# A decoder layer on one core: the last head's turn two row blocks later, its small steps in another order, and the gate sums one projection later

## Chip, cores and metric

The kernel runs on one core of a Trainium2 chip. The metric is the device time of one execution in microseconds (us). The kernel before took 787.35, 786.34 and 785.03 us in three runs, median 786.34.

## The reference

One layer maps 512 tokens of width 1024 to the same shape. A vector c gives six modulation rows (shift, scale and gate for two branches) through a 1024x6144 matrix. The first branch mixes tokens in two groups, whose outputs are joined and projected:

```
mod = silu(c) @ ada_w + ada_b               # 6 x 1024
u   = rms_norm(x) * (1 + scale) + shift
z   = u @ w_in                              # q, k, v, o, gates | a, b
# group 1: four mLSTM heads of width 256
lf  = log_sigmoid(f);  F = cumsum(lf);  m = running max(i - F)
s   = (q @ k.T) / 16 * exp(F_t - F_s + i_s - m_t)     # causal
h   = s @ v / max(|sum(s)|, exp(-m));  h = rms_norm(h) * sigmoid(o)
# group 2: GLU, causal depthwise convolution of width 31, layer norm, silu
y   = silu(layer_norm(conv(a * sigmoid(b))))
x1  = x + gate * rms_norm(concat(h, y) @ w_out)
# second branch: up to 2 x 2816, convolution of width 3, gated, down, gate
```

All is float32. Products are taken in three parts: each factor is split into a high and a low part (names ending in h and l), and high x high, low x high and high x low are added.

## The kernel before, in words

PE (TensorE) and SP (SyncE) work in the order in which the code is written. DVE (VectorE), ACT (ScalarE) and POOL (GpSimd) are ordered by a scheduler: it goes by priorities (raising `tc.cur_priority` by LATER makes what follows yield to the rest), by dependencies added by hand that only order two instructions on one engine (`add_manual_dep`, and `behind` for short), and inside `in_order()` by the code.

*Head 0 and the gates.* `head_proj(0, j)` (six calls) is one projection block of 24 products for q, k and o of the first head; the profile's products qko_0, qko_1 and so on. Between them stand the gate steps: `fcum` sums the log forget gates over tokens with eight small products (L752), DVE copies the sums (Fc, L754) and forms ga (L755), `aT` turns ga (L761), and DVE scans it. `g_lf`, which fcum reads, is the end of a chain of small DVE steps (L709 to L713) that stand between the convolution's taps (`cv`, L900). Those taps run on DVE through the whole first half.

*Head 3, the last.* `attention(h)` is a generator (L631 on) whose parts are put between other products by `next(steps)`: scores s (L639) and their scaling E on DVE (L640), the outputs o (L650), then per token tile a copy to hn and a sum of squares ssq on ACT. Then come the small steps, all 128x4: dm (L662), its reciprocal rd (L663), two steps on ssq (L664, L665) on DVE, ssq plus epsilon and its power fac on POOL (L666, L667), and for the last head fac times rd on DVE (L669). ACT scales hn by fac (L673, four copies), PE turns it (hT, L682: eight 128x128 transposes into two banks), and ACT and DVE split the turned rows into hh and hl (L692, L693).

*The output projection.* `mix_first(n)` multiplies row block n of w_out (wo_n, 128 rows, 12 products, n from 0 to 9) into the banks mixa; blocks 0 to 7 read the convolution group (yh, yl), blocks 8 and 9 the last head (hh, hl). The other heads go through products of sums (names m, ms, mt; Strassen-like) into mixa and mixb. Each raw block is loaded by SP; ACT makes the high part, POOL the low part (`w_split`, L199 and L200). After blocks 8 and 9 come wo1's ten blocks (the right half of the columns) into mixb.

*The modulation sums.* `ada_block(i)` loads a 128x1024 block of the transposed modulation matrix on ACT's queue (L177) and multiplies it by c with a sum along the row on DVE (`junk`, L182). 48 such blocks make mod; 20 to 39 are done while the last head and the output projection run. `gain` forms gains from mod; `send_rows` turns gains on PE (gT, L786), copies them on DVE (gTs, L789) and writes them to memory on ACT's queue (row_d, L791); `row` loads them back to all partitions (g1r, L797), after the write has landed. DVE multiplies mixa by g1r (mg).

Of the kernel before, what the change touches and what calls it, by code (L numbers as in the profile page):

```python
# [10 lines left out]
F32 = mybir.dt.float32  # L11
# [3 lines left out]
ALU = mybir.AluOpType  # L15
# [42 lines left out]
def decoder_layer(ctx, tc, w_glu0, x, c, adaT, vecs, w_glu, w_qko, w_v0, w_vo, w_mq, w_out, w_up, w_down, out):  # L58
# [46 lines left out]
    def atbank(name):  # L105
        return psum.tile([P, T], F32, tag="at", bufs=2, name=name)
# [63 lines left out]

    def ada_block(i, behind, load_behind=None):

        if i % 6 < 4 and 24 <= i < 40:
            r = spare[0][:, 2 * (i % 6) : 2 * (i % 6) + 2, :].rearrange("p j t -> p (j t)")
        else:
            r = adas.tile([P, D], F32, tag="ada", name=f"ada_{i}")
        load = nc.scalar.dma_start(r, adaT[i // 2][:, (i % 2) * D : (i % 2 + 1) * D])  # L177
        if load_behind is not None:
            tc.add_manual_dep(load.ins, load_behind.ins.name, mybir.DependencyInfo(mybir.DependencyClass.NoSync, mybir.DependencyReason.DATA),
                              reason="order on ScalarE")  # L180
        junk = small.tile([P, D], BF16, tag="junk", bufs=1, name=f"junk_{i}")
# [11 lines left out]
    def w_split(src, name, pool=None, tag="w", eng=None):  # L193

        n = src.shape[1]
        pool = pool or wpool
        hi = pool.tile([P, T], F32R, tag=tag, name=f"{name}h")
        lo = pool.tile([P, T], F32R, tag=tag, name=f"{name}l")
        S.activation(hi[:, :n], src, AF.Copy)  # L199
        last_w[0] = (eng or G).tensor_tensor(out=lo[:, :n], in0=src, in1=hi[:, :n].bitcast(F32), op=ALU.subtract)  # L200
        return hi, lo
# [363 lines left out]
    def head_proj(h, i):  # L565

        pieces, qs, ks, so = heads[h]
        ps = mmbank(f"qko{h}_{i}")
        proj(ps, pieces, i * KT)
        e = 2 * h + i % 2  # L570
        if i < 2:
            qs.append(conv4(ps, e, f"q{h}_{i}"))
        elif i < 4:
            ks.append(conv4(ps, 8 + e, f"k{h}_{i}"))
        else:
            t = slot(f"so{h}_{i}")
            S.activation(t, ps, AF.Tanh, scale=0.5)
            so.append(t)
# [49 lines left out]
        yield  # L628
        tc.cur_priority += LATER

    def attention(h):  # L631

        _, qs, ks, so = heads[h]

# [31 lines left out]
        G.tensor_scalar(out=ssq, in0=ssq, scalar1=EPS, scalar2=None, op0=ALU.add)  # L666
        last_fac[0] = G.tensor_tensor(out=fac, in0=ssq, in1=mhalf, op=ALU.pow)  # L667
        if h == H - 1:
            V.tensor_tensor(out=fac, in0=fac, in1=rd, op=ALU.mult)  # L669
# [6 lines left out]
        yield  # L676
        turned_h = []
        for e in range(2):
            tp = (mmbank if h < 2 else atbank)(f"hT{h}_{e}")
            for tt in range(NT):  # L680
                src = hn[tt // 2][:, (tt % 2) * DH + e * P : (tt % 2) * DH + (e + 1) * P]
                PE.transpose(tp[:, tt * P : (tt + 1) * P], src, ident)  # L682
# [9 lines left out]
            S.activation(hi, t, AF.Copy, scale=g)  # L692
            last_lo[0] = V.scalar_tensor_tensor(out=lo, in0=t, scalar=g, in1=hi.bitcast(F32), op0=ALU.mult, op1=ALU.subtract)  # L693
            hy[2 * h + e] = (hi, lo)
# [58 lines left out]
    Fc, ga = g16("Fc"), g16("ga")  # L753
    V.tensor_copy(Fc, fv)  # L754
    V.tensor_tensor(out=ga, in0=gz[:, :, :H], in1=Fc, op=ALU.subtract)  # L755
    head_proj(0, 2)

    head_proj(0, 3)
    aps = atbank("aT")
# [23 lines left out]
    def send_rows(a, n, queue=nc.scalar):  # L783

        ps = atbank(f"gT{a}")
        PE.transpose(ps[:n, :P], gains[:, a : a + n], ident)  # L786
        t = side(f"gTs{a}") if a == 3 * KT else slot(f"gTs{a}") if a == 0 else vpool.tile([P, 2 * T + 8], F32, tag="vh", name=f"gTs{a}")
        t = t[:, :P]
        V.tensor_copy(t[:n, :], ps[:n, :P])  # L789
        for i in range(n // KT):  # L790
            queue.dma_start(rows_d[a // KT + i].rearrange("(j p) -> j p", p=P), t[i * KT : (i + 1) * KT, :])  # L791
# [49 lines left out]

    def wo_split(r, n, i):
        wo[n + i] = w_split(r[:, i * T : (i + 1) * T], f"wo0_{n + i}")

    def mix_first(n, tts=range(NT)):
        if n not in wo:
# [18 lines left out]
            ts = slice(off + q * P, off + (q + 1) * P)  # L865
            mm3(ps, (hi[:, ts], lo[:, ts]), w[p], start and p == 0, p == PAIRS - 1, True)

    last_kept = [None]

    def kept(banks, name):  # L870
        out = [cvtile(f"{name}{q}") for q in range(2)]
        last_kept[0] = S.activation(out[0], banks[0], AF.Copy)
        V.tensor_copy(out[1], banks[1])
        return out

    ys = [None] * KT
# [102 lines left out]
    for h in range(H - 1):  # L979
# [48 lines left out]
        if h == H - 2:  # L1028
            norm_sums()

    tc.cur_priority += LATER
    for i in range(16, 20):
        ada_block(i, scaled)
    for i in range(20, 24):
        ada_block(i, last_left[0])
    ada_done(16, 24)
    gain(0, 16, "mix_post_g")
    tc.cur_priority -= LATER
    wo = {}
    steps = attention(H - 1)  # L1040
    low, high = mixa[:2], mixa[2:]
    s14 = upool.tile([P, KT, T], F32R, tag="uh", name="ms14")
    norm_factor()
# [41 lines left out]
        next(steps)  # L1085
    mix_first(0)
    next(steps)
    for p in range(PAIRS):
        sums_split(p, "14", (s14[:, 2 * p, :], s14[:, 2 * p + 1, :]))
    for n in range(1, 6):  # L1090
        mix_first(n)
    spare.append(upool.tile([P, KT, T], F32, tag="ul", name="spare"))
    for _ in steps:
        pass
    for i in range(24, 40):
        ada_block(i, last_yl[0], last_kept[0] if i < 28 else None)
# [12 lines left out]
    wt1 = right_load(mixq[1], "mt1")
# [513 lines left out]
```

## Time and profile before

| | before |
|---|---|
| median of three runs | 786.34 us |
| profiled execution | 784.7 us |
| its span | 783.0 us |
| mean granted TensorE clock | 0.988 |
| busy PE, DVE, POOL, ACT | 97%, 75%, 70%, 55% |
| PE waits for hT | 7.4 us, once |
| PE waits for fcum | 3.9 us, once |

The profile is that of one execution. A row of a timeline has the start in us from the span's start, the duration, engine, line, operation, output<-inputs by the program's names without their numbers, and in brackets the time in which the engine stood idle before it and what ended it. "x8" means eight instructions in one row. A row of the waits has who waited for whom, the sum, the times and the longest. The granted clock is TensorE's, 1.00 at full speed. ACTq and SPq are the queues that issue DMAs.

### The profile page before, as it was taken

How to read it: one execution, taken by the hardware profiler on the slowest of the kernel's cores; microseconds unless marked ns; L12 is line 12 of the kernel's file. 1: busy time of each engine (PE TensorE's matmuls, PEld its weight loads, DVE VectorE, ACT ScalarE, POOL GpSimd, SP SyncE). 2: the span in 40 equal slices, each digit the busy share in tenths (PEclk: the TensorE clock that was granted, in tenths of full speed). 3: DMA queues.
4: the chain of work that ended last, by engine and by line, in shares of the span. 5: the costliest groups of instructions: out<-in, count | busy, mean ns of one | idle time of the engine just before them, and what ended most of it. 6: DMA issues, size and time to landing. Idle time of an engine off the chain costs nothing.

```text
span 783.0 us, 10268 instructions
## 1 busy us (share of the span) xinstructions
PE 759.6 (97%) x3485; PEld 626.4 (80%) x3485; DVE 586.1 (75%) x863; ACT 429.7 (55%) x822; POOL 546.8 (70%) x447
## 2 busy tenths in 40 slices
PE   7999998999999999998799999999999999999996
PEld 5778896878788788786688988888888888888885
DVE  6669899979669796669947888875765677564538
ACT  7584427684665656583357744444444354557533
POOL 5779858895594953949661067986987784599944
PEclk9999998999999999999799999999999999999999
DMA  8994943321131341667674575766686573796364
GB/s 314 344 398 158 199 111 108 126 90 55 54 108 54 107 149 42 228 206 238 240 245 174 197 267 182 279 237 236 222 301 230 188 289 137 266 395 252 113 226 150
DMA packets 41976, 154.92 MB, mean 198 GB/s; under 512 B 3954, under 2 KB 5378, under 8 KB 32772
## 3 DMA queue, kind: packets, MB, share of 16 engines
q1 hardware_dynamic: 27764, 101.04, 36.2%
q10 hardware_dynamic: 12560, 50.08, 17.5%
q0 software_dynamic: 1600, 3.15, 2.4%
q8 instruction: 27, 0.44, 0.2%
q14 instruction: 25, 0.20, 0.1%
HBM read 134.19 MB, written 26.35 MB: 205 GB/s over the span
## 4 chain that ended last, share of the span: by engine, by line
PE 76%; DVE 9%; DMA 6%; issue 3%; ACT 3%; POOL 2%; ACTq 0%; DVEq 0%; SPq 0%; POOLq 0%
PE up L218 31%; PE qko L218 11%; PE dn L218 10%; PE vo L218 8%; PE glu L218 5%; DVE cv L900 3%; DMA wglu<-in_w_glu 3%; PE mixa L218 3%; PE mixb L218 2%; PE s L639 2%; PE o L650 2%; DVE junk L182 1%; DMA xr<-x1d 1%; PE glu L355 1%; DVE ydl L914 1%
## 5 line engine op out<-in xcount | busy, mean ns | idle before, releaser
L900 DVE SCALAR_TENSOR_TENSOR cv<-gt,cvw,cv 128x502 f32<-128x502 f32 (+23 forms) x200 | 136.9, 728 | 2.0 <-ACT cv L888 0.9
L896 POOL TENSOR_TENSOR cs<-cs,cs 128x510 f32<-128x510 f32 (+3 forms) x32 | 42.9, 1340 | 1.0 <-ACT cs L894 0.7
L200 POOL TENSOR_TENSOR wup_0l<-wup,wup_0h 128x512 fp32r<-128x512 f32 x18 | 27.0, 1498 | 19.1 <-ACT wup_0h L199 19.1
L182 DVE SCALAR_TENSOR_TENSOR junk<-ada,cb 128x1024 bf16<-128x1024 f32 x20 | 33.6, 1681 | 5.4 <-DMA ada<-in_adaT 5.3
L218 PE MATMUL up<-u2l,wup_512h 128*128 128x512 f32 (+1 forms) x96 | 35.7, 372 | 0.2 <-DVE u2l L1217 0.2
L218 PE MATMUL up<-u2h,wup_1024h 128*128 128x512 f32 (+1 forms) x96 | 35.8, 373 | 0.0
L218 PE MATMUL up<-u2h,wup_0h 128*128 128x512 f32 (+1 forms) x96 | 35.7, 372 | 0.0
L218 PE MATMUL up<-u2l,wup_0h 128*128 128x512 f32 (+1 forms) x96 | 35.7, 372 | 0.0
L218 PE MATMUL up<-u2h,wup_0l 128*128 128x512 f32 (+1 forms) x96 | 35.7, 372 | 0.0
L218 PE MATMUL up<-u2h,wup_512h 128*128 128x512 f32 (+1 forms) x96 | 35.6, 371 | 0.0
L218 PE MATMUL up<-u2h,wup_1536l 128*128 128x512 f32 (+1 forms) x96 | 35.6, 371 | 0.0
L218 PE MATMUL up<-u2h,wup_1536h 128*128 128x512 f32 (+1 forms) x96 | 35.6, 371 | 0.0
L218 PE MATMUL up<-u2l,wup_1536h 128*128 128x512 f32 (+1 forms) x96 | 35.6, 371 | 0.0
L218 PE MATMUL up<-u2h,wup_512l 128*128 128x512 f32 (+1 forms) x96 | 35.6, 371 | 0.0
L218 PE MATMUL up<-u2l,wup_1024h 128*128 128x512 f32 (+1 forms) x96 | 35.6, 371 | 0.0
L218 PE MATMUL up<-u2h,wup_1024l 128*128 128x512 f32 (+1 forms) x96 | 35.6, 371 | 0.0
L894 ACT ACTIVATE cs<-gt,cvw 128x511 f32<-128x511 f32 (+4 forms) x40 | 27.1, 712 | 6.5 <-POOL cs L896 2.6
L200 POOL TENSOR_TENSOR wup_1536l<-wup,wup_1536h 128x512 fp32r<-128x512 f32 x18 | 25.4, 1413 | 5.3 <-ACT wup_1536h L199 5.3
L1356 DVE TENSOR_TENSOR b<-b 128x512 f32<-128x512 f32 x11 | 19.4, 1762 | 9.4 <-POOL b L1355 9.4
L335 DVE SCALAR_TENSOR_TENSOR junk<-ada,cps 128x1024 bf16<-128x1024 f32 x16 | 19.5, 1219 | 9.1 <-DMA ada<-in_adaT 8.5
L199 ACT ACTIVATE wup_512h<-wup 128x512 fp32r<-128x512 f32 x22 | 13.8, 627 | 20.6 <-PE up L218 10.8
L1355 POOL TENSOR_TENSOR b<-b 128x512 f32<-128x512 f32 x11 | 14.7, 1332 | 13.9 <-DVE b L1354 10.2
(1261 smaller groups left out, 2803.1 us busy)
## 6 DMA issues: line engine op xcount, KB each, us to landing
wup<-in_w_up SPq DMA_DIRECT2D x22, 1024.0 KB, 5.4
b<-in_w_down ACTq DMA_DIRECT2D x11, 1024.0 KB, 6.5
spill_t<-b ACTq DMA_DIRECT2D x11, 1024.0 KB, 4.2
ada<-in_adaT ACTq DMA_DIRECT2D x20, 512.0 KB, 5.5
wqko<-in_w_qko SPq DMA_DIRECT2D x9, 1024.0 KB, 4.8
ada<-in_adaT SPq DMA_DIRECT2D x16, 512.0 KB, 7.4
wvo<-in_w_vo SPq DMA_DIRECT2D x6, 1024.0 KB, 4.8
spare<-in_adaT ACTq DMA_DIRECT2D x12, 512.0 KB, 5.9
```

Source lines behind the costliest of these rows:

```text
L182: t = V.scalar_tensor_tensor(out=junk, in0=r, scalar=1.0, in1=cb, op0=ALU.mult, op1=ALU.mult, accum_out=mod[:, i : i + 1])
L199: S.activation(hi[:, :n], src, AF.Copy)
L200: last_w[0] = (eng or G).tensor_tensor(out=lo[:, :n], in0=src, in1=hi[:, :n].bitcast(F32), op=ALU.subtract)
L218: PE.matmul(ps, l, r, start=start and i == 0, stop=stop and i == 2, skip_group_check=again)
L335: V.scalar_tensor_tensor(out=junk, in0=first[k][:, i * D : (i + 1) * D], scalar=1.0, in1=cps, op0=ALU.mult, op1=ALU.mult, accum_out=part[: ...
L639: PE.matmul(sp[:, :n], ks[d][:, cc * P : (cc + 1) * P], qs[d][:, cc * P :], start=d == 0, stop=d == 1)
L650: PE.matmul(o[:, : DH + 2], E[h][cc][:, a : a + P], vs[h][cc], start=cc == 0, stop=cc == tt)
L894: S.activation(t[:, d:], cvx[j][:, : T - d], AF.Copy, scale=w(CK - 1 - d))
L896: G.tensor_tensor(out=side[:, d:], in0=side[:, d:], in1=t[:, d:], op=ALU.add)
L900: tap = V.scalar_tensor_tensor(out=cp[:, d:], in0=cvx[j][:, : T - d], scalar=w(CK - 1 - d), in1=cp[:, d:], op0=ALU.mult, op1=ALU.add)
L1355: G.tensor_tensor(out=b12, in0=b22, in1=b12, op=ALU.subtract)
L1356: V.tensor_tensor(out=b22, in0=b22, in1=b11, op=ALU.subtract)
```

## The change

1. `head_proj(0, 2)` is called ahead of the gate sums instead of behind Fc and ga. PE's order goes from qko_1, fcum, qko_2, qko_3, aT to qko_1, qko_2, fcum, qko_3, aT.
2. The last step of `attention` for the last head (hT and what follows) is called behind `mix_first(7)` instead of behind `mix_first(5)`. Its two turned banks come from `cvbank` instead of `atbank`.
3. The splits of wo_6 and wo_7 on POOL are put behind fac.
4. The modulation sums 20 to 39 stand at other places on DVE, and their loads elsewhere on ACT's queue, in other buffers: one wide tile (`spare`, now allotted ahead of the last head) for 20 to 23 and 32 to 35, the tiles wide1 and wide2 for 30, 31 and 39, side tiles for 26 to 29. wide1 is loaded with g1r afterwards.

The core of the diff:

```diff
+        if n + i in (6, 7):
+            behind(last_w[0], last_fac[0])
...
-            tp = (mmbank if h < 2 else atbank)(f"hT{h}_{e}")
+            tp = (hbank or (mmbank if h < 2 else atbank))(f"hT{h}_{e}")
...
     head_proj(0, 1)
+    head_proj(0, 2)
 
     fps = atbank("fcum")
...
     V.tensor_tensor(out=ga, in0=gz[:, :, :H], in1=Fc, op=ALU.subtract)
-    head_proj(0, 2)
...
-    for i in range(20, 24):
+    for i in range(20, 22):
         ada_block(i, last_left[0])
-    ada_done(16, 24)
-    gain(0, 16, "mix_post_g")
     tc.cur_priority -= LATER
     wo = {}
-    steps = attention(H - 1)
+    steps = attention(H - 1, cvbank)
...
+    wide1, wide2 = (vpool.tile([P, 2 * T + 8], F32, tag="vh", name=f"wide{n}") for n in (1, 2))
+    tc.cur_priority += LATER
+    ada_block(22, last_kept[1])
+    for i in range(23, 25):
+        ada_block(i, last_yl[0])
+    ada_done(16, 24)
+    gain(0, 16, "mix_post_g")
+    tc.cur_priority -= LATER
...
-    for n in range(1, 6):
+    for n in range(1, 5):
         mix_first(n)
-    spare.append(upool.tile([P, KT, T], F32, tag="ul", name="spare"))
-    for _ in steps:
-        pass
-    for i in range(24, 40):
-        ada_block(i, last_yl[0], last_kept[0] if i < 28 else None)
-    ada_done(24, 40)
-    for n in range(6, NP - 2):
+    for n in range(5, NP - 2):
         mix_first(n)
         if n == 6:
             send_rows(0, KT)
+    tc.cur_priority += LATER
+    for i in range(25, 31):
+        ada_block(i, last_e[0])
+    tc.cur_priority -= LATER
+    for _ in steps:
+        pass
+    tc.cur_priority += LATER
+    for i in range(31, 40):
+        ada_block(i, last_lo[0])
+    ada_done(24, 40)
+    tc.cur_priority -= LATER
```

`last_e` is now also the last step on fac (L669), so sums 25 to 30 stand behind it. What follows is the order of the instructions in the two programs.

POOL, around the last head's two small steps (ssq3 and fac3), before. wo0_n are the row blocks of w_out, mt1 the factor of the first products into mixb; a name with l is a low part:

```order
L200 TENSOR_TENSOR wo0_5l_3511<-wo0_4_3504,wo0_5h_3510 128x512
L200 TENSOR_TENSOR wo0_6l_3515<-wo0_4_3504,wo0_6h_3514 128x512
L200 TENSOR_TENSOR wo0_7l_3519<-wo0_4_3504,wo0_7h_3518 128x512
L200 TENSOR_TENSOR mt1_0l_3665<-mt1_3660,mt1_0h_3664 128x512
L200 TENSOR_TENSOR mt1_1l_3669<-mt1_3660,mt1_1h_3668 128x512
L200 TENSOR_TENSOR mt1_2l_3673<-mt1_3660,mt1_2h_3672 128x512
L666 TENSOR_SCALAR ssq3_3357<-ssq3_3357 128x4
L667 TENSOR_TENSOR fac3_3450<-ssq3_3357,mhalf_109 128x4
L200 TENSOR_TENSOR wo0_8l_3695<-wo0_8_3662,wo0_8h_3694 128x512
```

The same place after:

```order
L207 TENSOR_TENSOR wo0_5l_3514<-wo0_4_3507,wo0_5h_3513 128x512
L673 TENSOR_SCALAR ssq3_3346<-ssq3_3346 128x4
L674 TENSOR_TENSOR fac3_3439<-ssq3_3346,mhalf_109 128x4
L207 TENSOR_TENSOR wo0_6l_3518<-wo0_4_3507,wo0_6h_3517 128x512
L207 TENSOR_TENSOR wo0_7l_3522<-wo0_4_3507,wo0_7h_3521 128x512
L207 TENSOR_TENSOR mt1_0l_3665<-mt1_3660,mt1_0h_3664 128x512
L207 TENSOR_TENSOR mt1_1l_3669<-mt1_3660,mt1_1h_3668 128x512
L207 TENSOR_TENSOR mt1_2l_3673<-mt1_3660,mt1_2h_3672 128x512
L207 TENSOR_TENSOR wo0_8l_3695<-wo0_8_3662,wo0_8h_3694 128x512
```

The two small steps moved ahead of five splits.

ACT, from the scaling of hn to the first split of m22 (the factor of a later product into mixb), before:

```order
L199 ACTIVATE wo0_8h_3694<-wo0_8_3662 128x512
L177 DMA spare_3546<-in_adaT 128x1024
L673 ACTIVATE hn3_0_3359<-hn3_0_3359,fac3_3450 128x256 x2
L673 ACTIVATE hn3_1_3360<-hn3_1_3360,fac3_3450 128x256 x2
L199 ACTIVATE wo0_9h_3698<-wo0_8_3662 128x512
L692 ACTIVATE hh3_0_3552<-hT3_0_3547,ghalf_141 128x512
L692 ACTIVATE hh3_1_3561<-hT3_1_3556,ghalf_141 128x512
L199 ACTIVATE wo1_0h_3708<-wo1_0_3706 128x512
L199 ACTIVATE wo1_1h_3712<-wo1_0_3706 128x512
L791 DMA row_d0_1429<-gTs0_3632 8x128
L199 ACTIVATE m22_0h_3718<-m22_3716 128x512
L797 DMA g1r_3657<-row_d0_1429 128x512 x2
```

And after, from the last splits ahead of hh (wide1 is now the tile of g1r):

```order
L206 ACTIVATE wo0_8h_3694<-wo0_8_3662 128x512
L206 ACTIVATE wo0_9h_3698<-wo0_8_3662 128x512
L206 ACTIVATE wo1_0h_3708<-wo1_0_3706 128x512
L206 ACTIVATE wo1_1h_3712<-wo1_0_3706 128x512
L798 DMA row_d0_1429<-gTs0_3563 8x128
L804 DMA wide1_3451<-row_d0_1429 128x512
L699 ACTIVATE hh3_0_3604<-hT3_0_3599,ghalf_141 128x512
L804 DMA wide1_3451<-row_d0_1429 128x512
L699 ACTIVATE hh3_1_3613<-hT3_1_3608,ghalf_141 128x512
L206 ACTIVATE m22_0h_3718<-m22_3716 128x512
```

wo1's two splits, the write of row_d and the loads of g1r moved ahead of hh.

DVE, from the copy Fc of the gate sums to ga, before (cv are the convolution's taps, q0 and k0 the short convolutions of q and k):

```order
L551 SCALAR_TENSOR_TENSOR q0_0c_1235<-qko0_0_1210,vec_111,q0_0c_1235 128x509
L754 COPY Fc_1277<-fcum_1272 128x16
L900 SCALAR_TENSOR_TENSOR cv3_1589<-gt0_622,cvw_140,cv3_1589 128x482
L551 SCALAR_TENSOR_TENSOR q0_1c_1266<-qko0_1_1241,vec_111,q0_1c_1266 128x511
L900 SCALAR_TENSOR_TENSOR cv4_1638<-gt4_771,cvw_140,cv4_1638 128x504
L755 TENSOR_TENSOR ga_1278<-gz_987,Fc_1277 128x16
```

And after:

```order
L558 SCALAR_TENSOR_TENSOR q0_1c_1266<-qko0_1_1241,vec_111,q0_1c_1266 128x509
L909 SCALAR_TENSOR_TENSOR cv4_1638<-gt4_771,cvw_140,cv4_1638 128x502
L762 COPY Fc_1308<-fcum_1303 128x16
L909 SCALAR_TENSOR_TENSOR cv4_1638<-gt4_771,cvw_140,cv4_1638 128x501
L763 TENSOR_TENSOR ga_1309<-gz_987,Fc_1308 128x16
L558 SCALAR_TENSOR_TENSOR k0_2c_1297<-qko0_2_1272,vec_111,k0_2c_1297 128x511
```

Fc moved behind seven more operations, and ga behind one instead of three after it. On DVE the last head's dm, rd, hn, both ssq and the step on fac now stand together behind sum 24; sums 25 to 30, the copy gTs and hl follow. The sums 31 to 39 stand between the later steps: 33 to 37 while POOL makes wo1's low parts, 38 and 39 behind the low parts of wup (the first factor of the second branch).

More of the change, by code (lines that the diff above doesn't have):

```diff
@@ L171, in ada_block @@
     def ada_block(i, behind, load_behind=None):
-        if i % 6 < 4 and 24 <= i < 40:
-            r = spare[0][:, 2 * (i % 6) : 2 * (i % 6) + 2, :].rearrange("p j t -> p (j t)")
+        if 20 <= i < 24 or 32 <= i < 36:
+            q = 2 * (i % 4)
+            r = spare[0][:, q : q + 2, :].rearrange("p j t -> p (j t)")
+        elif 26 <= i < 30:
+            if i % 2 == 0:
+                spare.append(side(f"ada_{i}"))
+            r = spare[-1][:, (i % 2) * D : (i % 2 + 1) * D]
+        elif i in (30, 31, 39):
+            r = (wide1 if i == 30 else wide2)[:, :D]
         else:
@@ L629, in urgent, with attention @@
         tc.cur_priority += LATER
-    def attention(h):
+    def attention(h, hbank=None):
         _, qs, ks, so = heads[h]
@@ L668, in attention @@
         if h == H - 1:
-            V.tensor_tensor(out=fac, in0=fac, in1=rd, op=ALU.mult)
+            last_e[0] = V.tensor_tensor(out=fac, in0=fac, in1=rd, op=ALU.mult)
         for tt in range(NT):
@@ L866, in mix_product @@
             mm3(ps, (hi[:, ts], lo[:, ts]), w[p], start and p == 0, p == PAIRS - 1, True)
-    last_kept = [None]
+    last_kept = [None, None]
     def kept(banks, name):
@@ L872, in kept @@
         last_kept[0] = S.activation(out[0], banks[0], AF.Copy)
-        V.tensor_copy(out[1], banks[1])
+        last_kept[1] = V.tensor_copy(out[1], banks[1])
         return out
@@ L1029, in decoder_layer @@
             norm_sums()
+    spare.append(upool.tile([P, KT, T], F32, tag="ul", name="spare"))
     tc.cur_priority += LATER
@@ L1105, in decoder_layer @@
     x1 = [x1[2 * tt : 2 * tt + 2] for tt in range(NT)]
-    wide1 = vpool.tile([P, 2 * T + 8], F32, tag="vh", name="g1r")
     g1r = row(0, lambda n: [wide1[:, :T], wide1[:, T : 2 * T]], "g1")
```

## The prediction

> **What bounds the kernel now.** The page's busy line and then the waits of PE come first.
>
> ```profile
> PE 759.6 (97%) x3485; PEld 626.4 (80%) x3485; DVE 586.1 (75%) x863; ACT 429.7 (55%) x822; POOL 546.8 (70%) x447
> PE hT L682 <- ACT hn L673: 7.4, 1, 7.4
> PE fcum L752 <- DVE g_lf L713: 3.9, 1, 3.9
> PE s L639 <- DVE E L640: 1.0, 1, 1.0
> ```
>
> TensorE is the bound: busy 97% of the span, and only where it waits can time be won. Its two longest waits are one each at the places that the change touches: the last head's turn (hT, 7.4 us) and the gate sums (fcum, 3.9 us). But a wait also costs after it has ended. The windows below show, after the stretch, its length, PE's busy time and matmuls, four engines' busy times, and then the granted clock, DMA share and GB/s.
>
> ```profile
> 126.68:130.09 3.41, 0.95 (x5) 0.44 (x3) 3.41 (x6) 1.89 (x4) 1.97 (x2) 1.00 0.68 279
> 130.09:133.51 3.42, 1.99 (x9) 1.99 (x10) 3.42 (x7) 3.42 (x7) 3.42 (x4) 0.50 0.02 5
> 328.06:331.47 3.41, 2.95 (x15) 2.52 (x16) 1.96 (x6) 1.50 (x3) 3.41 (x4) 1.00 0.83 314
> 369.02:372.43 3.41, 0.00 (x0) 0.00 (x0) 3.38 (x4) 0.00 (x0) 3.33 (x3) 1.00 0.71 243
> 372.43:375.85 3.42, 0.00 (x0) 0.00 (x0) 3.35 (x8) 0.78 (x2) 3.03 (x3) 0.50 0.62 190
> 375.85:379.26 3.41, 3.00 (x10) 2.25 (x11) 3.34 (x5) 3.20 (x7) 1.89 (x2) 0.50 1.03 390
> 379.26:382.67 3.41, 3.41 (x9) 2.64 (x9) 3.41 (x5) 1.29 (x3) 3.28 (x3) 0.50 0.81 274
> ```
>
> In these rows the clock changes at the edges of 3.41 us windows. A window in which PE was busy 0.95 us (28%) is followed by half clock; one with 2.95 us (86%) is not; and half clock lasts through the first full window. So each long wait is followed by some 3 to 7 us of work at half speed.
>
> **The turn.** PE's timeline around the last head's turn (start, length, operation, in brackets the idle time before and what ended it):
>
> ```profile
> 368.51 0.39 PE L218 MATMUL mixa<-wo_5h,yl 128*128 128x512 f32 x1
> 376.26 2.53 PE L682 MATMUL hT<-ident,hn 128*128 128x128 f32 x8 [7.37 <-ACT hn L673]
> 378.44 0.78 PE L218 MATMUL mixa<-wo_6h,yh 128*128 128x512 f32 x1
> 386.12 0.39 PE L218 MATMUL mixb<-mt_0h,ms 128*128 128x512 f32 x1
> 390.20 0.39 PE L218 MATMUL mixa<-wo_8h,hh 128*128 128x512 f32 x1
> 395.64 0.39 PE L218 MATMUL mixb<-wo_0h,yh 128*128 128x512 f32 x1
> 418.77 1.03 PE L1191 MATMUL xT<-ident,un 128*128 128x128 f32 x8
> ```
>
> From the end of row block 5 (368.51 + 0.23) to the first product with mt (386.12) pass 17.4 us. In them lie 24 products and 8 transposes. At full clock 24 products take 5.44 us, as the 24 from 390.20 to 395.64 do, and eight transposes some 0.9 (the last row's 1.03 less the drain of its last one). So the wait and its slow clock cost 17.4 − 6.4 = **11.0 us**. What PE waited for is a chain of small operations of which each stands behind a large one:
>
> ```profile
> 359.62 1.24 DVE L662 TENSOR_TENSOR dm<-dm,em 128x4 f32<-128x4 f32 x1
> 368.18 1.23 DVE L665 TENSOR_TENSOR ssq<-ssq,rd 128x4 f32<-128x4 f32 x1
> 360.80 2.35 POOL L200 TENSOR_TENSOR wo_6l<-wo,wo_6h 128x512 fp32r<-128x512 f32 x1
> 369.35 2.32 POOL L200 TENSOR_TENSOR mt_2l<-mt,mt_2h 128x512 fp32r<-128x512 f32 x1
> 372.92 1.99 POOL L667 TENSOR_TENSOR fac<-ssq,mhalf 128x4 f32<-128x4 f32 x1
> 375.70 1.71 ACT L673 ACTIVATE hn<-hn,fac 128x256 f32<-128x256 f32 x4 [0.56 <-DVE fac L669]
> ```
>
> On DVE sums stand ahead of dm, of either ssq and of fac; on POOL the two steps wait behind five splits (wo_6l to mt_2l, 360.80 to 371.67).
>
> *After.* no sum stands on DVE from dm to fac, and two instead of three ahead of dm, so dm starts at 359.62 at the latest. Six short operations follow to the second ssq, of 1.24 us at most beside POOL: they end between 360 and 367. POOL turns to its two steps right behind wo_5l (ended 360.8); with 1.99 for fac and 1.71 for hn the turn's input is there between 364 and 371. PE now has two row blocks more to do before it asks: 368.74 + 5.44 = 374.2. That leaves 3 us of slack or more, and the 11.0 us go. **Term 1: −11.0** (−9 if a transpose still waits a little; no reason lets it grow).
>
> **What is late next: row block 8.** It needs hh, the scaled turn. PE now gets there at 374.2 + 0.9 + 4.08 (mt's products, 386.12 to 390.20) = 379.2. On ACT hh used to follow hn at once; now it stands behind wo1's first two splits, the write of row_d (the transposed gains) and the load back of it, which waits for that write to land. Before, that pair stood behind hh:
>
> ```profile
> 384.78 0.53 ACTq L791 DMA_DIRECT2D row_d<-gTs  x1
> 389.32 1.00 ACTq L797 DMA_DIRECT2D g1r<-row_d  x2
> 390.37 0.63 ACT L199 ACTIVATE m_1h<-m 128x512 fp32r<-128x512 f32 x1 [4.30 <-issue]
> 377.98 0.69 ACT L692 ACTIVATE hh<-hT,ghalf 128x512 fp32r<-128x512 f32 x1
> wo<-in_w_out SPq DMA_DIRECT2D x1, 512.0 KB, 5.7
> DMA to landing us min/median/max: 3.1/3.3/3.4
> ```
>
> The second issue came 4.54 us after the first, and m_1h sat idle behind it for 4.30 us. The last two rows are the landing of wo1's first load (issued at 371.7) and of the 256 KB loads of g1r. In the new order: the load of wo1 goes out when mt_2l is done, at about 372; it takes 3.1 to 5.7 us; I take 4.3, between the two. Its two splits (0.62 each) end at 377.5. DVE's copy gTs stands behind six sums: 6 × 2.2 us beside POOL from 361.5 gives 375, so it isn't last. row_d then needs 3.1 (g1r's best, a larger transfer) to 4.54 us, the first half of g1r 0.35 to issue, hh 0.69: 381.6 to 383.0 against PE's 379.2. **A new wait of 2.4 to 3.8 us; I take 3.2.** With a slower wo1 load it is 5; with both fast it is near 0.5.
>
> A wait of 3.2 us need not fill a window. By the rows, 28% busy is enough for half clock, 86% is not; where this wait falls against the edges isn't known, so it is even whether half clock follows, which costs 2.8 us (worked out below at fcum: 10.3 − 3.6 − 3.9). I put 1.4 into the sum. **Term 2: +4.6** (0.5 to 8.6). The Trainium skill (TensorE: Matmul & The Clock Gate, "HAM oscillation — how this bites in real kernels") sets the bound at idle gaps above about 3.4 us; this case's trace is stricter, since 2.46 us of idleness inside one window did it. By that rule alone this term would be 3.2 and the sum 1.4 us lower.
>
> **The gate sums.** PE and DVE before:
>
> ```profile
> 127.24 0.39 PE L218 MATMUL qko<-uh,wqko_1536l 128*128 128x512 f32 x1
> 131.52 0.61 PE L752 MATMUL fcum<-g_lf,tri 128*128 128x16 f32 x2 [3.89 <-DVE g_lf L713]
> 137.80 0.39 PE L218 MATMUL qko<-uh,wqko_512h 128*128 128x512 f32 x1
> 138.54 1.27 DVE L755 TENSOR_TENSOR ga<-gz,Fc 128x16 f32<-128x16 f32 x1
> 141.70 1.51 DVE L900 SCALAR_TENSOR_TENSOR cv<-gt,cvw,cv 128x502 f32<-128x502 f32 x2
> ```
>
> From 127.47 to 137.80, 10.3 us pass for fcum (0.9 at full clock) and 12 products (2.72): 6.7 us of cost, 3.9 of it idle and 2.8 slow clock. With the sums one projection later (24 products, 5.44 us), PE comes to fcum at 132.9; g_lf was done at 131.5, and the wait is gone. But aT, one projection further, needs ga, and DVE now has Fc behind the tap of width 502 and ga behind that of 501: 141.70 + 0.65 − 1.27 (ga no longer ahead) = 141.1 for Fc, 142.0 to 143.1 for ga. PE is at aT at 132.9 + 0.9 + 5.44 = 139.3 and waits 2.8 to 3.8 us. Of the 6.7 us, 3.3 stay as a wait, and a stretch at half clock (up to 2.8, 2.0 taken) may follow it again. **Term 3: −1.4** (−3.5 to +0.2).
>
> **E behind a load.** ACT's last copy out of vo, and E's second block on DVE:
>
> ```profile
> 321.34 0.39 ACT L527 ACTIVATE so<-vo 128x256 f32<-128x256 f32 x1
> 327.92 0.55 DVE L640 SCALAR_TENSOR_TENSOR E<-s,E 128x384 f32<-128x384 f32 x1
> ```
>
> The sums 20 to 23 now alternate with the last head's four E on DVE, and sum 20's buffer is loaded only after that copy (ended 321.7). With the 5.7 us of the load of the same size above, the load ends at 327.4 and the sum at 328.6; E's second block stands behind it, 0.7 us later than before, and each further sum may add as much. PE's wait at s (1.0 us) grows. **Term 4: +0.9** (0 to 2.5).
>
> **Given back later.** The last split that POOL makes for this part and the product that reads it, and the last step ahead of xT on DVE:
>
> ```profile
> 403.07 1.30 POOL L200 TENSOR_TENSOR wo_9l<-wo,wo_9h 128x512 fp32r<-128x512 f32 x1
> 410.15 0.39 PE L218 MATMUL mixb<-wo_9l,hh 128*128 128x512 f32 x1
> 415.95 0.48 DVE L1181 TENSOR_SCALAR un<-x,rf0r 128x512 f32<-128x512 f32 x1
> ```
>
> PE came to wo_9l 5.8 us after POOL had made it (404.37 to 410.15), and to xT 2.3 us after un (416.43 to 418.77). By terms 1 to 4 it comes 6.9 us earlier. POOL gains too (it doesn't wait for ACT any more at wo_8l), but sums 33 to 37 now run beside its last splits, and a split beside a sum took 2.35 (wo_6l) against 1.30 (wo_9l): up to 5 × 1.05 back. In front of un stand sums 38 and 39 and the gains on DVE. I put 1 us to each place. **Term 5: +2.0** (0 to 5).
>
> The sum: −11.0 + 4.6 − 1.4 + 0.9 + 2.0 = **−4.9 us**. The profiled execution took 784.7 (span 783.0, 1.7 around it), 1.6 below the median of 786.34; the sum takes it to 779.8 and the median to **781.4**. Behind xT PE shows only 0.2 us of waits, so what is left there reaches the end.
>
> **The rivals.**
> - *All gained.* wo1 and row_d land at their fastest and the later slacks hold: −11.0 + 0.5 − 1.4 + 0.9 + 0.7 = −10.3, 776.0. For it: POOL no longer waits for ACT; against it: ACT did wait 4.3 us for row_d.
> - *No measurable change.* Row block 8 waits 5.8 us with half clock (8.6), term 3 is −0.5, term 4 is +1.5: with −11.0 and no further give-back −1.4, near 785. For it: the 4.54 and 5.7 us rows as they stand.
> - *Slower.* gTs is the last to come: the six sums ahead of it wait for loads in a stretch in which the DMA engines are busy 0.7 to 1.0. To lose 2.4 us, term 2 has to reach 11.9, that is a wait of 9.1 with half clock: hh ready at 388.3, gTs no earlier than 382.5 instead of 375. Each of two sums would have to find its load 4 us late. Price +3, 789.
> - *It does not do what it says:* sums 23 and 24, ahead of dm, wait so long for their loads that hT waits as before. That takes 6 us of lateness; counted with no change.
>
> **How the numbers follow.** Forecast 0.50 (781.4, by itself 777.5 to 783.5), all gained 0.17, no change 0.18 and 0.03, slower 0.12. A measurement of this kernel tells about 0.3% (2.4 us) from no change: faster 0.67, same 0.21, slower 0.12. The range runs from below the second case to just short of the slower one, 775.0 to 787.8.
>
> **What would show it.** Right: no wait at hT, fcum gone from the waits with one of 3 us at aT, and one of 2 to 5 us at the products of wo_8h with hh, released by ACT. Wrong: hT still waiting over 1 us (term 1), no wait at wo_8h (term 2), or waits above 4 us together behind 395 us.

## The result, and the profile after

| | before | after |
|---|---|---|
| median (16 runs each) | 786.23 us | 781.72 us |
| lowest to highest | 784.08 to 788.16 | 777.56 to 785.45 |
| ratio after/before, 95% interval | | 0.9944 [0.9925, 0.9963] |
| profiled execution (its span) | 784.7 (783.0) | 781.7 (780.0) |

The kernel is 4.5 us faster, and the interval stays clear of 1. The forecast was 781.4. The total came out; whether its terms did is another matter. PE's waits after the change (who waited for whom, sum, times, longest):

```profile
PE mixa L225 <- ACT hh L699: 3.4, 1, 3.4
PE aT L768 <- DVE ga L763: 3.3, 1, 3.3
...
PE xT L1211 <- ACT un L1203: 2.8, 1, 2.8
```

hT (7.4), fcum (3.9) and E (1.0) are gone from the list. Three waits of about 3 us stand in their place: at hh, at aT and, later, at xT. PE's timeline at the marks that the prediction used, with a bracket where PE stood idle:

```profile
364.50 0.39 PE L225 MATMUL mixa<-wo_5h,yl 128*128 128x512 f32 x1
...
370.31 1.03 PE L689 MATMUL hT<-ident,hn 128*128 128x128 f32 x8
371.10 0.47 PE L225 MATMUL mixb<-mt_0h,ms 128*128 128x512 f32 x1
378.85 0.50 PE L225 MATMUL mixa<-wo_8h,hh 128*128 128x512 f32 x1 [3.39 <-ACT hh L699]
386.36 0.39 PE L225 MATMUL mixb<-wo_0h,yh 128*128 128x512 f32 x1
401.80 0.50 PE L225 MATMUL mixb<-wo_9l,hh 128*128 128x512 f32 x1 [0.71 <-POOL wo_9l L207]
413.48 1.27 PE L1211 MATMUL xT<-ident,un 128*128 128x128 f32 x8 [2.77 <-ACT un L1203]
436.44 0.36 PE L225 MATMUL up<-u2h,wup_1024h 128*128 128x256 f32 x1
```

Three marks of before that were not shown yet: the first product ahead of the last head, the head's first output o, and the product of the up projection that follows the last of the four turns xT, one for each token tile (up products of the earlier tiles stand between these turns).

```profile
319.49 0.95 PE L224 MATMUL ry_s<-ones,ysq 128*128 128x1 f32 x8
343.65 1.03 PE L650 MATMUL o<-v,E 128*128 128x258 f32 x4
439.44 0.36 PE L218 MATMUL up<-u2h,wup_1024h 128*128 128x256 f32 x1
```

And the first two of them after:

```profile
316.91 0.95 PE L231 MATMUL ry_s<-ones,ysq 128*128 128x1 f32 x8
339.43 1.47 PE L657 MATMUL o<-v,E 128*128 128x258 f32 x6
```

Subtracting start from start shows where along PE's program time was won and lost:

| mark | before | after | shift | gained or lost since the mark above |
|---|---|---|---|---|
| ry_s | 319.49 | 316.91 | −2.6 | −2.6: the gate sums, and the spread told below |
| first o | 343.65 | 339.43 | −4.2 | −1.6: the last head's scores |
| end of row block 5 | 368.74 | 364.73 | −4.0 | +0.2 |
| first product with mt | 386.12 | 371.10 | −15.0 | −11.0: the turn |
| first wo_0h into mixb | 395.64 | 386.36 | −9.3 | +5.7: hh |
| first xT | 418.77 | 413.48 | −5.3 | +4.0: POOL, then un |
| up behind the fourth xT | 439.44 | 436.44 | −3.0 | +2.3: half clock behind xT, and the later turns |

From the end of row block 5 to up behind the fourth xT pass 70.70 us before and 71.71 after. In this profile the 11.0 us of the turn were given back in full, between row block 8 and the fourth xT. What arrives at the end was won ahead of row block 5.

The windows of after, laid on the edges at which the clock changes (columns as in the prediction: length, busy time of PE, its loads, DVE, ACT and POOL, granted clock, DMA share, GB/s):

```profile
137.79:141.20 3.41, 0.77 (x4) 0.30 (x2) 3.41 (x7) 3.40 (x7) 3.41 (x4) 1.00 0.81 308
141.20:144.61 3.41, 2.73 (x9) 2.10 (x10) 3.41 (x7) 1.92 (x4) 3.41 (x4) 0.50 0.01 2
...
376.74:380.15 3.41, 1.24 (x4) 0.76 (x5) 1.31 (x2) 2.04 (x4) 0.17 (x1) 1.00 0.71 237
380.15:383.56 3.41, 3.41 (x9) 2.63 (x9) 3.38 (x4) 2.21 (x5) 3.41 (x3) 0.50 0.69 255
```

Behind either wait, aT's and hh's, one window runs at half clock. That costs 1.4 us at aT, half of the 2.73 in which PE works there, and 1.7 at hh. The coin that the prediction tossed at hh (even whether half clock follows) fell on the costly side, though PE had been busy 1.24 us (36%) of that window.

**Who held hh.** ACT's queue and timeline at that place, after:

```profile
373.49 0.63 ACT L206 ACTIVATE wo_0h<-wo 128x512 fp32r<-128x512 f32 x1 [6.02 <-DMA wo<-in_w_out]
373.66 0.53 ACTq L798 DMA_DIRECT2D row_d<-gTs  x1
377.71 0.36 ACTq L804 DMA_DIRECT2D wide<-row_d  x1
378.11 0.69 ACT L699 ACTIVATE hh<-hT,ghalf 128x512 fp32r<-128x512 f32 x1 [3.47 <-DMA row_d<-gTs]
```

It is the chain that the prediction named: wo1's load (wo_0h starts at 373.49, predicted: the splits end at 377.5), the write of row_d, 4.05 us until its load back goes out (predicted 3.1 to 4.54), hh. wo1 came earlier than forecast, but so did PE.

How long the write of row_d took decides whether PE waits here. In after, SP had issued a load of 768 KB 0.27 us ahead of it:

```profile
373.39 0.33 SPq L864 DMA_DIRECT2D m<-in_w_mq  x1
```

The DMA engines were 61% busy until the load back went out. In the profiles of f1 and a4 (told below, with the same code at this place) the write at 375.94 and 374.53 came 0.6 us ahead of that load, the engines were 2% busy, the load back went out after 1.24 us, and PE did not wait for hh. In three profiles the load back followed after 4.05 to 4.54 us, with the engines 56% to 61% busy and a load issued on SP 0.3 to 1.3 us ahead (before, a1, after); in seven after 1.23 to 1.24, with 2% to 24%. That the other load delays the write is read from these rows; no run tested it.

**Who held xT.** SP's queue, POOL, ACT and DVE after:

```profile
400.03 1.72 POOL L207 TENSOR_TENSOR wo_9l<-wo,wo_9h 128x512 fp32r<-128x512 f32 x1
401.77 0.33 SPq L1245 DMA_DIRECT2D wup<-in_w_up  x1
406.73 0.63 ACT L206 ACTIVATE wup_0h<-wup 128x512 fp32r<-128x512 f32 x1 [7.06 <-DMA wup<-in_w_up]
...
407.79 0.57 ACT L819 ACTIVATE mixb0junk<-mixb 128x512 bf16<-128x512 f32 x1
412.70 0.72 ACT L1203 ACTIVATE un<-x,rf0r 128x512 f32<-128x512 f32 x1 [0.39 <-POOL rf0r L828]
```

The same place on ACT before, where a second split follows the first as it does after:

```profile
409.30 0.63 ACT L199 ACTIVATE wup_0h<-wup 128x512 fp32r<-128x512 f32 x1 [2.15 <-DMA wup<-in_w_up]
...
410.86 0.60 ACT L812 ACTIVATE mixb0junk<-mixb 128x512 bf16<-128x512 f32 x1 [0.41 <-PE mixb L218]
```

mixb0junk, the sum of squares of the finished first tile, opens the chain that ends in un and xT. Before, it waited for PE (0.41 us). After, PE had finished that tile at 402.4, and ACT could not start on it before 407.79. It stood behind two splits of the second raw block of the up weights. That block is loaded into the buffer that POOL frees with wo_9l: the SP issue at 401.77 follows POOL's end at 401.75, and landing took 5 us. PE came 8.35 us earlier to wo_9l (410.15 to 401.80), the load only 2.6 us earlier (409.30 to 406.73).

### The profile page after: what moved, and what is told of

It reads as the page before. It is cut to its first block, busy times and chain, and to the rows that moved or that the text cites. A ratio compares the mean times of both kernels' runs of the same rounds, so it can differ in the third digit from the quotient of the medians.

```text
span 780.0 us, 10257 instructions
## 1 busy us (share of the span) xinstructions
PE 758.9 (97%) x3485; PEld 626.0 (80%) x3485; DVE 592.0 (76%) x863; ACT 428.3 (55%) x822; POOL 545.3 (70%) x447
## 4 chain that ended last, share of the span: by engine, by line
PE 79%; DVE 7%; POOL 5%; issue 3%; DMA 2%; ACT 2%; DVEq 0%; SPq 0%; ACTq 0%; POOLq 0%
PE up L225 31%; PE dn L225 13%; PE qko L225 10%; PE vo L225 8%; PE glu L362 4%; PE mixa L225 4%; DVE cv L909 3%; PE s L646 2%; PE glu L225 2%; PE o L657 2%; DMA wglu<-in_w_glu 1%; DVE ydl L923 1%; PE mixb L225 1%; DMA xn<-in_x 1%; DMA row_d<-gTs 1%
## 5 line engine op out<-in xcount | busy, mean ns | idle before, releaser
L189 DVE SCALAR_TENSOR_TENSOR junk<-ada,cb 128x1024 bf16<-128x1024 f32 x21 | 36.1, 1718 | 2.1 <-DMA ada<-in_adaT 1.7
L206 ACT ACTIVATE wup_512h<-wup 128x512 fp32r<-128x512 f32 x22 | 13.8, 627 | 20.8 <-PE up L225 12.7
```

## The experiments

Every experiment was timed against before in five rounds, and its ratio is that to before on the same chip, whose median was 786.44 (a1, b1, a3, a4), 785.37 (f1, c2, c1, d1) and 786.91 (c3, e2); medians are not compared across these groups. A single profile varies: ry_s stands between 316.9 and 321.9 us in the twelve profiles, with waits of 3.3 to 4.2 us at aT and 3.9 to 5.1 at fcum, wherever these stand. The nine with the new order of the gates have ry_s at 319.3 on average, the three with the old at 320.4, so the −2.6 of the table above is not by itself what the gate sums brought. For this reason spans of single profiles are not compared. The table uses the timed ratio and, from each profile, the **stretch** from the end of row block 5 to up behind the fourth xT. The stretch varies too: f1 and after share its code and differ by 3.2 us, so a smaller difference shows nothing by itself.

| kernel | median us | ratio [95%] | stretch us |
|---|---|---|---|
| before | 786.23 | | 70.70 |
| after | 781.72 | 0.9944 [0.9925, 0.9963] | 71.71 |
| a1: gate sums alone | 782.59 | 0.9952 [0.9936, 0.9969] | 70.78 |
| f1: all but the gate sums | 784.31 | 0.999 [0.9974, 1.0006] | 68.55 |
| b1: turn alone | 784.78 | 0.9987 [0.9969, 1.0005] | 70.67 |
| a3: after, hh ahead of g1r | 783.75 | 0.9957 [0.9941, 0.9974] | 69.93 |
| a4: after, up splits behind the chain | 782.72 | 0.9956 [0.9932, 0.998] | 69.02 |
| c2: a4, five sums earlier | 781.70 | 0.996 [0.9943, 0.9978] | 69.63 |
| c1: c2 with a3 | 781.85 | 0.9955 [0.9938, 0.9972] | 69.06 |
| d1: c2 with the turn back behind block 5 | 784.55 | 0.9974 [0.9948, 1.0] | 70.78 |
| c3: a3, a4, two sums earlier behind gTs | 779.74 | 0.9923 [0.9893, 0.9953] | 66.77 |
| e2: c3 without sums 33 to 39 | 777.53 | 0.9896 [0.9869, 0.9923] | 64.08 |

### a1, f1: the gate sums against all the rest

a1 is before with `head_proj(0, 2)` ahead of the gate sums. f1 is after with it back behind them:

```diff
     head_proj(0, 1)
-    head_proj(0, 2)
...
     V.tensor_tensor(out=ga, in0=gz[:, :, :H], in1=Fc, op=ALU.subtract)
+    head_proj(0, 2)
```

a1:

> The kernel before with only the gate sums one projection later. Theory: the wait at fcum (3.9 us) goes, one of 3 us at aT comes, and the half clock behind it is shorter, so PE stands 2.0 to 2.8 us ahead of before at 320 us and keeps it, since nothing else changes: ratio 0.9965 to 0.9975. Rival: the wait only moves, or the 2.6 us seen at 317 us in the changed kernel come from elsewhere: 1.0000 within 0.0008.

f1:

> The changed kernel with the gate sums back in their old place, so that only the turn, the small steps and the modulation sums differ from before. Theory: from the end of row block 5 to the first product with up the changed kernel takes 71.7 us against 70.7 before, so the turn gains nothing, and what is left is the 1.6 us that PE saves at the last head's scores: ratio 0.9975 to 0.9995. Rival (the prediction's terms: -11.0 + 4.6 + 0.9 + 2.0 = -3.5): 0.9955 within 0.001.

a1 gives 0.9952, 3.8 us, which is more than its theory said and most of what the whole change gives; f1 gives 0.999, as its theory said, not to be told from 1. Together 0.9952 × 0.999 = 0.9942, the whole change's 0.9944. PE's two longest waits in a1 show that the turn was untouched:

```profile
PE hT L682 <- ACT hn L673: 7.5, 1, 7.5
PE aT L761 <- DVE ga L756: 3.3, 1, 3.3
```

The turn, the small steps and the sums together bring about 1 us, which is not told from nothing. f1's stretch is 3.2 us shorter than after's with the same code in it (its profiled execution, 782.12 us, was 2.2 below its median). In f1's profile PE did not wait for hh, and waited at xT all the same:

```profile
PE xT L1211 <- ACT un L1203: 3.3, 1, 3.3
```

So hh is late in some executions and not in others.

### b1: the turn alone

Before, with the turn behind `mix_first(7)` and in other banks; the sums and the small steps stay.

```diff
-    steps = attention(H - 1)
+    steps = attention(H - 1, cvbank)
...
-    for _ in steps:
-        pass
...
             send_rows(0, KT)
+    for _ in steps:
+        pass
```

> The kernel before with only the last head's turn behind row block 7 and in the other banks; small steps, sums and gates as before. Theory (a later chain takes the gain): the wait at hT falls from 7.4 to about 2 us and PE stands some 8 us ahead at the first product with mt, but POOL still ends wo_9l at 404.4 and the second load of wup still goes out then, so un is ready at 416.4 as before: xT starts at 416.4 to 417, and the end is 1.0 to 2.3 us earlier, ratio 0.997 to 0.9987. Rival (each wait counts for itself): 6 to 8 us earlier, 0.990 to 0.9925.

0.9987 and a stretch of 70.67: nothing that can be told from 1. The wait at hT is down to 2.0 us, and PE has a new one:

```profile
PE mixb L218 <- DVE gTs L789: 4.6, 1, 4.6
```

DVE at that place:

```profile
383.66 2.16 DVE L182 SCALAR_TENSOR_TENSOR junk<-spare,cb 128x1024 bf16<-128x1024 f32 x1
385.75 0.28 DVE L789 COPY gTs<-gT 8x128 f32<-8x128 f32 x1
```

The size was as expected, the place was not: no wait at xT, but one at the products with mt. Their second tile uses the bank that gT left, and gTs, the copy that frees it, stands on DVE behind the sums. Before, that copy was hidden under the wait at hT. The turn by itself uncovers the next holder within 6 us.

### a3, a4: one new wait taken away at a time

a3 puts the load back of g1r behind hh on ACT:

```diff
-            S.activation(hi, t, AF.Copy, scale=g)
+            last_hh[0] = S.activation(hi, t, AF.Copy, scale=g)
...
-    g1r = row(0, lambda n: [wide1[:, :T], wide1[:, T : 2 * T]], "g1")
+    g1r = [wide1[:, :T], wide1[:, T : 2 * T]]
+    for hf, r in enumerate(g1r):
+        behind(nc.scalar.dma_start(r, rows_d[0][hf * T : (hf + 1) * T].partition_broadcast(P)), last_hh[0])
```

> The changed kernel with the loads of g1r behind hh on ACT. Theory (a later chain takes the gain): the 3.4 us wait at wo_8h falls under 1 us and no half clock follows, so PE is some 5 us further at the first product of mixb with wo_0h; POOL's wo_9l and the second load of wup stay where they are (401.8), so PE waits 4 to 5 us at wo_9l and xT starts at 413 to 413.5 as now: within 0.001 of the changed kernel's ratio of 0.9944. Rival (each wait counts for itself): 4.5 to 5.7 us faster than the changed kernel, 0.987 to 0.989.

The wait at hh is gone, and with it the half clock, and the time stays (0.9957), as the theory said. ACT in a3, at the same place as above:

```profile
410.61 0.63 ACT L206 ACTIVATE wup_0h<-wup 128x512 fp32r<-128x512 f32 x1 [7.92 <-DMA wup<-in_w_up]
...
411.67 0.58 ACT L819 ACTIVATE mixb0junk<-mixb 128x512 bf16<-128x512 f32 x1
```

The splits still stand ahead of mixb0junk, and PE waited 5.0 instead of 2.8 us at xT. What hh had cost was paid there instead (the theory had put it at wo_9l, where PE waited 0.7 us).

a4 leaves hh as it is and moves three splits of the second up block, and the load after them, behind the first tile's chain:

```diff
-        for _ in range(2):
-            up_split(1, raw1, slots, "t")
...
-        up_split(1, raw1, slots, "t")
...
-        raw2 = raw_up(2)
...
+        for _ in range(3):
+            up_split(1, raw1, slots, "t")
+        raw2 = raw_up(2)
```

> The changed kernel with the first three splits of the second block of wup behind the first token tile's chain (mixb's square sum, x, un) instead of ahead of it. Theory: ACT's square sum of mixb0 stood behind the split that waits for the load of wup (406.7); now it starts at 403, DVE takes the factor when sum 39 is done (406.5) instead of at 408.6, un is ready at about 411, the wait at xT falls from 2.8 us to under 1 and the half clock behind it goes: 2.5 to 4 us faster than the changed kernel, ratio 0.9895 to 0.9915. Rival (sums 38 and 39 on DVE hold the chain): xT still waits over 2 us, ratio 0.994.

The rival was right: xT still waits 2.7 us. ACT and DVE in a4:

```profile
400.51 0.57 ACT L819 ACTIVATE mixb0junk<-mixb 128x512 bf16<-128x512 f32 x1
...
403.30 1.23 DVE L189 SCALAR_TENSOR_TENSOR junk<-ada,cb 128x1024 bf16<-128x1024 f32 x1 [1.43 <-DMA ada<-in_adaT]
...
406.33 0.20 DVE L826 TENSOR_SCALAR rm0t<-msq 128x1 f32<-128x1 f32 x1
```

Counted from the end of row block 5, mixb0junk now runs 9.4 us earlier than in after (33.6 us behind it, not 43.1), and its next step on DVE (rm0t) stands behind sums 38 (shown) and 39 (at 404.57), the first of which waited 1.43 us for its load. So xT had two holders, one close behind the other: ACT with the splits, and DVE with the last sums, which is enough by itself.

### c2, c1, d1: earlier sums

c2 is a4 with five of the nine last sums (31 to 35) moved ahead of the splits of the turned rows:

```diff
-    for i in range(25, 31):
+    for i in range(25, 36):
         ada_block(i, last_e[0])
...
-    for i in range(31, 40):
+    for i in range(36, 40):
         ada_block(i, last_lo[0])
```

> The changed kernel with the splits of the second block of wup behind the first token tile's chain and the sums 31 to 35 behind the step on fac (so that 31 to 39 all stand ahead of wup's first low parts on DVE). Theory (two holders of the chain to xT, ACT's splits and DVE's sums 38 and 39, and both are gone now): no wait over 1 us at xT and no half clock behind it; the wait at wo_8h stays 3 to 5 us. The projection stretch falls from 71.7 to 66 to 68 us: ratio 0.988 to 0.991. Rival (POOL's splits, or a load, hold PE at the next place): stretch over 70, ratio 0.994 to 0.996.

xT no longer waits, as the theory said, but the ratio of 0.996 is the rival's. PE's longest wait in c2 is another:

```profile
PE mixb L225 <- DVE gTs L796: 5.7, 1, 5.7
```

It is b1's holder again. The copy runs 12.7 us behind the end of row block 5 (at 381.25), in after 6.2 us behind it (at 370.90), since more sums stand ahead of it.

c1 adds a3's edit:

> As the run before, and the loads of g1r behind hh on ACT. Theory: with the chain to xT free the 3.4 us at wo_8h and the half clock behind it (2.1) now count: a stretch of 61 to 64 us, 4 to 5.5 us less than the run before, ratio 0.982 to 0.986. Rival (POOL's splits wo_7l to wo_9l hold PE): at most 1.5 us faster than the run before, and a wait of 3 us or more at them.

0.9955, so the theory's gain did not come; the wait for gTs stays at 5.8 us. Neither theory nor rival had it at that place.

d1 is c2 with the turn back in its old place:

```diff
+        if n == 5:
+            for _ in steps:
+                pass
...
-    for _ in steps:
-        pass
```

> As the run c1, but with the turn back behind row block 5 (hh then stands ahead of the write of row_d by itself; the small steps keep their new place). Theory (it is the place of the small steps that freed the turn, not its later place): hn is ready 3 us ahead of PE, no wait at hT over 0.5 us, and the time is within 0.002 of the run c1. Rival (the later place is needed): a wait of 3 us or more at hT and 4 us or more slower than c1.

PE's timeline in d1 has no wait at hT, right behind row block 5:

```profile
369.95 1.03 PE L689 MATMUL hT<-ident,hn 128*128 128x128 f32 x8
```

So it is the small steps' new place on DVE and POOL that frees the turn; the two row blocks of delay are not needed for it. What follows is the wait for gTs, 6.9 us, and 0.9974 [0.9948, 1.0], which is told neither from c1 nor, clearly, from before.

### c3, e2: all holders at once, and what still holds

c3 takes a3's and a4's edits, and of the sums moves only 31 and 32, behind the copy gTs instead of ahead of it:

```diff
-        V.tensor_copy(t[:n, :], ps[:n, :P])
+        last_gts[0] = V.tensor_copy(t[:n, :], ps[:n, :P])
...
-    for i in range(25, 31):
-        ada_block(i, last_e[0])
+    for i in range(25, 33):
+        ada_block(i, last_e[0] if i < 31 else last_gts[0])
```

> The changed kernel with three edits: the loads of g1r behind hh on ACT, the first three splits of the second block of wup behind the first token tile's chain, and the sums 31 and 32 behind the copy gTs (so that gTs and with it the bank of mixb1 come no later than in the changed kernel, and the sums 33 to 39 come two places earlier). Theory: no wait over 1.5 us at mixb1, wo_8h or xT, and no half clock between row block 5 and xT; the projection stretch falls from 71.7 us to 62 to 66: ratio 0.984 to 0.989. Rival (POOL's splits of wo1 beside the sums hold PE): waits of 3 us or more in all at wo_2l to wo_9l, stretch 67 to 69, ratio 0.990 to 0.994.

0.9923 [0.9893, 0.9953], 779.74 us from six runs: the lowest ratio here with the whole computation. It is clear of before; from after it is not told, since the intervals overlap. The stretch falls to 66.77 us. The longest waits left in it:

```profile
PE mixb L225 <- POOL wo_8l L207: 1.2, 1, 1.2
PE mixa L225 <- DVE hl L700: 0.8, 1, 0.8
```

and POOL's last two splits, with the last sum on DVE:

```profile
397.98 2.18 DVE L189 SCALAR_TENSOR_TENSOR junk<-wide,cb 128x1024 bf16<-128x1024 f32 x1
399.04 2.25 POOL L207 TENSOR_TENSOR wo_8l<-wo,wo_8h 128x512 fp32r<-128x512 f32 x1
401.25 1.27 POOL L207 TENSOR_TENSOR wo_9l<-wo,wo_9h 128x512 fp32r<-128x512 f32 x1
```

The ratio lies in the rival's range (0.990 to 0.994): POOL is the holder now, and its splits take 2.25 beside a sum, 1.27 without. But PE's waits for POOL are 1.7 us in all (0.5 at wo_7l), not the rival's 3. And the theory's "no half clock" failed: from 397.94 to 401.35 PE was busy 48%, and the next 3.4 us ran at half clock, which costs 1.7.

e2 is c3 with the modulation sums 33 to 39 and their loads left out and those columns of mod set to zero, so the gains that use them are not the reference's:

```diff
-    for i in range(33, 40):
-        ada_block(i, last_lo[0])
...
+    V.memset(mod[:, 33:40], 0.0)
```

> As the run before, with the modulation sums 33 to 39 and their loads left out (those columns are set to zero instead). Theory of the give-back (sums on DVE beside POOL's splits): POOL's splits of wo1 take 1.3 us each instead of 1.3 to 2.4, wo_9l is ready 3 us earlier or more, and the waits that the run before still has behind row block 8 fall under 1 us in all: 2 to 5 us faster than the run before. Rival (the sums cost nothing there, PE is held by products alone): within 1 us of the run before.

The same two splits in e2:

```profile
394.46 1.29 POOL L208 TENSOR_TENSOR wo_8l<-wo,wo_8h 128x512 fp32r<-128x512 f32 x1
395.71 1.29 POOL L208 TENSOR_TENSOR wo_9l<-wo,wo_9h 128x512 fp32r<-128x512 f32 x1
```

PE no longer waits for POOL in this stretch, and no part of it runs at half clock; PE waits 2.2 us once, for DVE's hl (0.8 in c3). The stretch is 2.7 us shorter than in c3, the ratio 0.9896 against 0.9923 (on one chip, with intervals that overlap, so the gain itself is not shown). What the rows do show is that with the sums goes the near doubling of POOL's splits (their loads are left out too, but c3 by itself has the same contrast, 2.25 against 1.27). The Trainium skill (SBUF — State Buffer, "SBUF: two separate sides") says that VectorE and GpSimd share one pair of ports, which whichever starts first holds for its whole instruction; among the VectorE operations that this concerns it has those with two SBUF inputs, against a GpSimd operation that reads SBUF. The rows agree: 1.29 alone, 2.25 when a sum of 1.2 us takes its turn in between.

## Why the prediction was right, and where its steps were not

Direction and median were right: 781.4 against 781.72. That the median came so close is luck, as the terms show. In the profile the sum was −4.9 and −3.0 came (784.7 to 781.7); the medians differ by −4.5, since the profiled execution of before was a short one for its kernel. Three of the five terms were off.

1. **The turn, −11.0.** Exact: 386.12 − 368.74 = 17.4 us became 371.10 − 364.73 = 6.4. hn was ready at 361.25, PE asked at 370.31. d1 shows that the turn needed only the small steps' new place. The tail of the term, "what is late next", decided what it is worth.
2. **hh behind row_d, +4.6.** Mechanism right, and the size within its range: 3.4 us of wait, 1.7 of half clock and 0.6 of smaller delays, 5.7 in all. But f1 and a4 show executions in which PE does not wait there. The term's 3.1 us at the least for row_d, taken from the loads of g1r, was no lower bound: the write took 1.24 there. And a3 shows that removing the wait gives nothing that can be measured, since xT waits longer in its place. The term was added as if it stood by itself; terms 2 and 5 are one behind the other, and only the later counts.
3. **The gate sums, −1.4.** Mechanism right: fcum's wait gone, one of 3.3 at aT (forecast 2.8 to 3.8), one window of half clock behind it (PE was busy 80% of that window and full clock followed, where the prediction had half clock last through the first full window). The size was too small. By the rows, the 6.7 us of before became 3.3 of wait and 1.4 of half clock (2.0 was taken), which is −2.0; up to ry_s it is −2.6 in the profile, and timed in a1 −3.8 ([−5.0, −2.4] by its interval), against a range of −3.5 to +0.2. The 1.8 us between −2.0 and −3.8 are less than what single profiles of one order differ by ahead of ry_s (316.9 to 321.7 with the new one); the runs don't say more.
4. **E behind a load, +0.9.** Wrong in sign: −1.6. The step that failed is "sum 20's buffer is loaded only after that copy". ACT and DVE after:

```profile
317.12 0.34 ACTq L184 DMA_DIRECT2D spare<-in_adaT  x1
318.85 0.45 ACTq L184 DMA_DIRECT2D spare<-in_adaT  x1
319.78 0.39 ACT L534 ACTIVATE so<-vo 128x256 f32<-128x256 f32 x1
321.86 1.48 DVE L189 SCALAR_TENSOR_TENSOR junk<-spare,cb 128x1024 bf16<-128x1024 f32 x1 [1.45 <-DMA spare<-in_adaT]
323.28 0.55 DVE L647 SCALAR_TENSOR_TENSOR E<-s,E 128x384 f32<-128x384 f32 x1
```

   The loads go out before the last copies out of vo (so, 319.78), sum 20 runs at 321.86 instead of the 327.4 that I had worked out (2.6 us of that is the shift at ry_s), and PE's wait at s is gone.

5. **Given back later, +2.0.** Named at the right two places, wo_9l and xT, and sized a third of what this profile shows: +6.3 (4.0 to the first xT, 2.3 behind). I had put 1 us at xT for sums 38 and 39 on DVE. I did not follow the buffer that wo_9l frees: the next load of the up weights waits for it, ACT's splits for the load, and the chain to xT behind them on ACT. It fell outside its own range (0 to 5). The total stood because terms 3 and 4 erred the other way: −1.2 and −2.5 against +4.3 here and +1.1 at term 2.

So the total was right with a wrong account: the forecast had the turn pay and the gates add a little. Timed, the gates pay 3.8 us and the rest about 1 (f1: between −2.0 and +0.5). Of the rivals, "no measurable change" is what happened to the turn itself (f1: 0.999), by another way than the one described: not a wait of 5.8 us at row block 8, but one shared out between hh, wo_9l and xT.

What stays open: how a1's gain beyond the 2.0 us that the rows carry comes about, and why executions of the same code differ as after and f1 do. The rows show what differs: row_d's write (4.05 us against 1.24) and wo1's first split, 8.8 us behind row block 5 in after and 7.5 in f1 and a4. The cause of either was not tested.

## What to carry to other kernels

A wait on the critical engine hides whatever becomes ready while it lasts: before pricing its removal, list every later consumer in the same stretch, with the time at which its input is ready, and count the gain only up to the first that isn't earlier too. Follow buffers as well as instructions: the last reader of a buffer starts the next load, and the engine that handles that load may be the one on which the next critical step stands in line. Waits one behind another are not added: taking one or two away (a3, a4, c2) gave nothing that could be measured. With hh and both holders of xT out of the way, and gTs no later (c3), the ratio fell from after's 0.9944 to 0.9923, which the intervals don't tell apart; that they have to go together is argued, not shown.

## What the runs showed of the hardware

- DMA issues on ACT's queue ran ahead of activations that stand before them in the program. The order of ACT after has the loads into spare behind the last v and so:

```
L533 ACTIVATE v3_2904<-vo3_3_3013 128x256
L534 ACTIVATE so3_1_2907<-vo3_3_3013 128x256
L184 DMA spare_3101<-in_adaT 128x1024 x6
```

  Four of the loads were issued at 317.12 to 318.85, the first right behind the last product of vo (ended 317.08); the last copy, `so`, ran at 319.78. An issue that itself has to wait does hold back what follows: the load back of g1r did so for hh (3.47 us).
- The 4 KB write of row_d and the issue of the load back that waits for it lay 1.23 to 1.24 us apart with the DMA engines 2% to 24% busy, and 4.05 to 4.54 with 56% to 61% (figures under "Who held hh").
- A wait of 2.77 us (xT) was enough for a window at half clock, as these windows of after show:

```profile
410.80:414.20 3.40, 0.72 (x7) 0.72 (x8) 1.56 (x6) 2.78 (x8) 0.55 (x1) 1.00 0.97 318
414.20:417.60 3.40, 3.40 (x12) 2.72 (x11) 2.27 (x5) 1.45 (x4) 0.59 (x2) 0.51 0.69 274
373.33:376.74 3.41, 2.13 (x10) 1.44 (x8) 0.00 (x0) 1.16 (x2) 2.54 (x3) 1.00 0.65 211
```

  With the rows shown with the result, a window with PE busy 21% to 36% was followed by half clock three times out of three, for one window each; so was the one with 48% in c3, where two waits of 0.5 and 1.2 us were enough. The one with 62% (last row) was not. The wait at fcum, by whose window the prediction called this trace stricter, lasted 3.9 us as a whole; those at aT and xT here were shorter, 3.3 and 2.8.
